# Softmax over 32768 columns: uniform 32 KB chunks, and 896 columns of one late chunk in transfers of seven partitions

## The chip, the core and the metric

The kernel runs on one core of one Trainium2 chip. The metric is the device time of one execution in microseconds; the median of three executions stands for a kernel.

## The reference

```python
batch, seq, vocab = 16, 256, 32768
logits: float32 [16, 256, 32768], temperature = 1.0

scaled = logits / temperature
scaled = scaled - scaled.max(axis=-1, keepdims=True)
exp_scaled = np.exp(scaled)
return (exp_scaled / exp_scaled.sum(axis=-1, keepdims=True)).astype(np.float32)
```

There are 4096 rows of 32768 numbers. 536.87 MB are read and as many are written.

## The kernel before

**Tiling.** Each row is cut into two halves of 16384 columns, and each half sits on a partition of its own, so two neighbouring partitions hold one row. 128 half rows are a group, and there are G = 64 groups. A group is loaded, worked on and stored in two chunks of 8192 columns (`_CW`), each 128 partitions x 32 KB, 4 MB. Six chunk buffers (`X`, `_BUFS`) form a ring, so three groups are in SBUF at a time: group g uses buffers `slots(g)`, that is 2g and 2g + 1 modulo 6.

**Work on a group** (class `Half`). `vector()` runs on VectorE (DVE): for each piece it waits for the load and takes the negated maximum (L123). `scalar()` runs on ScalarE (ACT): it takes the exponential in place and sums it (L168). Then a short chain joins the pieces and the two partitions of a row: a shuffle that swaps neighbours (L134), a minimum (L138), a small exponential (L179), a multiply-add (L142), a reciprocal (L153). At last VectorE scales each piece in place (L157), and a store is issued as soon as its piece is scaled (`stores`).

**Queues.** SyncE (SP) issues all loads, and waits on `st[b]` before it fills a buffer again, until the store of the group before has landed. ScalarE's queue issues the stores of groups 0 to 60 (`stores(act, ...)`), SyncE those of groups 61 to 63. Both queues feed the same 16 DMA engines.

**Edges.** The first and the last group are loaded by `load_edge` in pieces of 4096 columns (`_EDGE`, rows of 16 KB, 2 MB a transfer, L98), all others by `load` (L90). `first()` works on group 0 in whole chunks and waits for both edge pieces of a chunk. `last(G - 1)` works on, and stores, the last group in four pieces of 4096 columns. Groups 1 to 60 run in a loop of `turns` = 20 turns of three groups on VectorE and ScalarE; the rest is written out. All stores go through line L103. At the end SyncE waits for all stores (L255).

The order of SyncE around the change, at the end:

```python
    for c in range(2):
        sp.wait_ge(st[c], (turns + 1) * 16)
        load_edge(G - 1, c, c)
...
    for g in range(G - 3, G):
        last(g).stores(sp, g)
...
    for b in range(_BUFS):
        sp.wait_ge(st[b], total[b])
```

## Time and profile before

| | |
|---|---|
| median of 3 executions | 2488.16 us (2488.12 to 2488.49) |
| the profiled execution: time, span | 2488.27 us, 2486.5 us |
| VectorE busy | 1724.6 us, 69% |
| ScalarE busy | 944.5 us, 38% |
| maximum of a chunk (L123), 126 of 128x8192 | 8.68 us each |
| exponential of a chunk (L168), 126 of 128x8192 | 7.12 us each |
| scaling of a chunk (L157), 126 of 128x8192 | 4.54 us each (mean) |
| 4 MB load, issue to landing (median) | 26.5 us |
| 4 MB store by ScalarE's queue, issue to landing (median) | 48.3 us |
| 4 MB store by SyncE's queue, issue to landing (median) | 33.7 us |

Times in the profile are microseconds from the start of the span. Engines are PE, DVE (VectorE), ACT (ScalarE), POOL (GpSimd) and SP (SyncE); a "q" behind the name (SPq, ACTq) is the engine's sequencer, which waits and issues transfers. L123 is a line of the kernel's file. In a group of instructions, out<-in are the program's names, followed by partitions x elements and type, and xN is how many there are. "Share" or tenths of DMA is the mean over the 16 DMA engines. A transfer of 128 partitions is cut into one packet per row, eight on each engine; each engine writes a four-byte record to the transfer's semaphore when its part is done, so a completion consists of sixteen.

### The profile page before, as it was taken

How to read it: one execution, taken by the hardware profiler on the slowest of the kernel's cores; microseconds unless marked ns; L12 is line 12 of the kernel's file. 1: busy time of each engine (PE TensorE's matmuls, PEld its weight loads, DVE VectorE, ACT ScalarE, POOL GpSimd, SP SyncE). 2: the span in 40 equal slices, each digit the busy share in tenths (PEclk: the TensorE clock that was granted, in tenths of full speed). 3: DMA queues.
4: the chain of work that ended last, by engine and by line, in shares of the span. 5: the costliest groups of instructions: out<-in, count | busy, mean ns of one | idle time of the engine just before them, and what ended most of it. 6: DMA issues, size and time to landing. Idle time of an engine off the chain costs nothing.

```text
span 2486.5 us, 2019 instructions
## 1 busy us (share of the span) xinstructions
DVE 1724.6 (69%) x644; ACT 944.5 (38%) x325; POOL 0.2 (0%) x4
## 2 busy tenths in 40 slices
DVE  6777767767677676676766767667676676766764
ACT  3444333343333433434334343343433434334342
POOL 0000000000000000000000000000000000000000
DMA  9999999999999999999999999999999999999999
GB/s 413 430 435 433 430 438 431 430 438 431 432 436 431 436 432 431 438 430 432 437 430 434 435 430 438 431 430 438 431 432 436 431 436 432 431 438 431 430 437 399
DMA packets 37730, 1073.77 MB, mean 432 GB/s; under 512 B 4192, under 2 KB 4192, under 8 KB 4192
## 3 DMA queue, kind: packets, MB, share of 16 engines
q1 hardware_dynamic: 20160, 562.05, 52.4%
q10 hardware_dynamic: 17568, 511.71, 47.7%
q14 instruction: 2, 0.02, 0.0%
HBM read 536.87 MB, written 536.87 MB: 432 GB/s over the span
## 4 chain that ended last, share of the span: by engine, by line
DMA 58%; DVE 18%; another core or an unknown queue 14%; ACT 8%; issue 1%; SPq 0%; ACTq 0%; DVEq 0%
DMA out_dram<-xs 37%; DMA xs<-in_logits_dram 21%; DVE t L123 11%; ACT xs L168 7%; DVE xs L157 6%; SPq L90 0%; ACT ee L179 0%; DVE t L134 0%; DVE row L153 0%; DVE row L138 0%; DVE junk L142 0%; ACTq L103 0%; SPq L98 0%; DVEq L133 0%
## 5 line engine op out<-in xcount | busy, mean ns | idle before, releaser
L168 ACT ACTIVATE xs<-xs,t 128x8192 f32<-128x8192 f32 (+1 forms) x130 | 912.1, 7016 | 1468.4 <-DVE t L123 1468.4
L123 DVE TENSOR_REDUCE t<-xs 128x1 f32<-128x8192 f32 (+1 forms) x130 | 1110.8, 8551 | 234.0 <-DMA xs<-in_logits_dram 234.0
L157 DVE TENSOR_SCALAR xs<-xs,ee,row 128x8192 f32<-128x8192 f32 (+1 forms) x130 | 576.5, 4478 | 2.3
L134 DVE LOAD_MASK_SELECT t<-t x64 | 0.9, 14 | 470.3 <-ACT xs L168 470.3
L179 ACT ACTIVATE ee<-t,row 128x4 f32<-128x4 f32 x64 | 19.0, 298 | 35.9 <-DVE row L138 35.9
L142 DVE CUSTOM_DVE_ANT_1 junk<-ee,t 128x4 f32<-128x4 f32 x64 | 10.4, 163 | 23.3 <-ACT ee L179 23.3
L168 ACT ACTIVATION_READ_ACCUMULATOR xs<-xs,t 128x1 f32 x130 | 24.3, 187 | 0.0
L153 DVE RECIPROCAL row<-row 128x1 f32<-128x1 f32 x64 | 10.5, 164 | 2.2
L138 DVE TENSOR_REDUCE row<-t 128x1 f32<-128x4 f32 x64 | 10.1, 157 | 2.2
L134 DVE STREAM_SHUFFLE t<-t 128x4 f32<-128x4 f32 x64 | 10.2, 160 | 0.6
L142 DVE DVE_READ_ACCUMULATOR2_ANT row<- 128x1 f32 x64 | 5.3, 82 | 0.0
L168 ACT ACT_TABLE_LOAD x1 | 1.3, 1283 | 0.9 <-SPq L54 0.9
L272 POOL MEMSET const-bfloat16-1.0<- 128x1 bf16 x1 | 0.1, 102 | 0.0
L272 POOL MEMSET const-uint8-127<- 128x1 uint8 x1 | 0.1, 101 | 0.0
L272 POOL MEMSET const-float32-0.0<- 128x1 f32 x1 | 0.1, 99 | 0.2 <-issue 0.2
L272 POOL MEMSET const-float32-1.0<- 128x1 f32 x1 | 0.1, 98 | 0.0
## 6 DMA issues: line engine op xcount, KB each, us to landing
xs<-in_logits_dram SPq DMA_DIRECT2D x124, 4096.0 KB, 26.5
out_dram<-xs ACTq DMA_DIRECT2D x122, 4096.0 KB, 48.3
xs<-in_logits_dram SPq DMA_DIRECT2D x8, 2048.0 KB, 16.1
out_dram<-xs SPq DMA_DIRECT2D x4, 4096.0 KB, 33.7
out_dram<-xs SPq DMA_DIRECT2D x4, 2048.0 KB, 21.9
```

The costliest lines, as they stand in the source:

```text
L123: m = dve.tensor_reduce(out=t[:, k : k + 1], in_=xcols(self.slots[c], s, w), axis=X_, op=A.max, negate=True)
L134: dve.stream_shuffle(out=t[:, 2 * K : 4 * K], in_=t[:, 0 : 2 * K], mask=swap).then_inc(site(tag, "sh"), 1)
L138: dve.tensor_reduce(out=r[:, 0:1], in_=tv[:, :, 0, :], axis=XY, op=A.min).then_inc(site(tag, "mx"), 1)
L142: dve.tensor_tensor_reduce(out=j[:, 0 : 2 * K].rearrange("p (a k) -> p a k", a=2), in0=e[:, 0 : 2 * K].rearrange("p (a k) -> p a k", a=2), ...
L153: dve.reciprocal(out=r[:, 2:3], in_=r[:, 1:2]).then_inc(site(tag, "rc"), 1)
L157: dve.tensor_scalar(out=xs, in0=xs, scalar1=e[:, k : k + 1], scalar2=r[:, 2:3], op0=A.mult, op1=A.mult).then_inc(site(tag, "sc", k), 1)
L168: a = act.activation(out=xs, in_=xs, func=Exp, bias=t[:, k : k + 1], scale=inv_t, accum_out=t[:, K + k : K + k + 1],)
L179: act.activation(out=e[:, 0 : 2 * K].rearrange("p (a k) -> p a k", a=2), in_=tv[:, :, 0, :], func=Exp, bias=r[:, 0:1], scale=-1.0,).then_i ...
L272: nc = _bacc.Bacc("TRN2", target_bir_lowering=False, num_devices=1)
```

## The change

- `load_edge`, `first`, `last` and the pieces of 4096 columns go. All groups are loaded, worked on and stored in whole chunks of 8192 columns.
- The loop of VectorE takes in group 0 and runs 21 turns (groups 0 to 62), then group 63 alone. ScalarE's loop runs 20 turns (groups 0 to 59), and groups 60 to 63 are written out; the store of group 60 stays on its queue.
- SyncE stores groups 61 to 63 as before, but the first chunk of group 62 is split: columns 0 to 7295 go in one transfer of 128 partitions, and columns 7296 to 8191 (896 columns, 3584 B a row) in 19 transfers, 18 of seven partitions and one of two. They have a semaphore of their own (`few`), which only the end waits for.
- The waits at the end stand in another order.

```diff
-_EDGE = 4096
+_FEW = 7
+_FEWCOLS = 896
...
-    turns = (G - 4) // _SETS
+    turns = G // _SETS
...
     for g in range(_SETS):
         for c in range(2):
-            (load_edge if g == 0 else load)(g, c, slots(g)[c])
-    with sp.Fori(1, turns + 1) as i:
+            load(g, c, 2 * g + c)
+    with sp.Fori(1, turns) as i:
         for b in range(_BUFS):
             sp.wait_ge(st[b], i * 16)
             load(i * _SETS + b // 2, b % 2, b)
     for c in range(2):
-        sp.wait_ge(st[c], (turns + 1) * 16)
-        load_edge(G - 1, c, c)
+        sp.wait_ge(st[c], turns * 16)
+        load(G - 1, c, c)
...
     with dve.Fori(1, turns + 1) as i:
         for q in range(_SETS):
-            turn(q, i).vector()
-    for g in range(G - 3, G):
-        last(g).vector()
+            Half(q, i).vector()
+    Half(0, turns + 1).vector()
...
+    last = [(G - 4 + q, Half(q % _SETS, turns + q // _SETS)) for q in range(4)]
+    for g, h in last:
+        h.scalar()
+        if g == G - 4:
+            h.stores(act, g)
...
+    few = nc.alloc_semaphore("few")
+    n_few = 0
+    for g, h in last[1:]:
+        if g != G - 2:
+            h.stores(sp, g)
+            continue
+        sp.wait_ge(site(h.tag, "sc", 0), h.n)
+        b, cut = h.slots[0], _CW - _FEWCOLS
+        sp.dma_start(
+            out=o[bass.ds(g * P, P), 0:cut], in_=X[:, b * _CW : b * _CW + cut]
+        ).then_inc(st[b], 16)
+        for p in range(0, P, _FEW):
+            n = min(_FEW, P - p)
+            sp.dma_start(
+                out=o[bass.ds(g * P + p, n), cut:_CW], in_=X[p : p + n, b * _CW + cut : (b + 1) * _CW]
+            ).then_inc(few, 16)
+            n_few += 1
+        sp.wait_ge(site(h.tag, "sc", 1), h.n)
+        store(sp, g, 1, h.slots[1])
+    sp.wait_ge(few, 16 * n_few)
+    for b in [2, 3, 4, 5, 0, 1]:
+        sp.wait_ge(st[b], 16 * len(range(b, 2 * G, _BUFS)))
```

More of the change, by code (lines that the diff above doesn't have):

```diff
@@ L49 @@
     G = N * 2 // P
-    turns = (G - 4) // _SETS
-    assert turns * _SETS + 4 == G and _BUFS == 2 * _SETS
+    turns = G // _SETS
+    assert turns * _SETS + 1 == G and _BUFS == 2 * _SETS
     swap = [i ^ 1 for i in range(32)]
@@ L55 @@
     X = nc.alloc_sbuf_tensor("xs", [P, _BUFS * _CW], fp32)
-    KM = 4
+    K = 2
     sets = [
         Set(
-            nc.alloc_sbuf_tensor(f"t{q}", [P, 4 * KM], fp32),
-            nc.alloc_sbuf_tensor(f"ee{q}", [P, 2 * KM], fp32),
-            nc.alloc_sbuf_tensor(f"junk{q}", [P, 2 * KM], fp32),
+            nc.alloc_sbuf_tensor(f"t{q}", [P, 4 * K], fp32),
+            nc.alloc_sbuf_tensor(f"ee{q}", [P, 2 * K], fp32),
+            nc.alloc_sbuf_tensor(f"junk{q}", [P, 2 * K], fp32),
             nc.alloc_sbuf_tensor(f"row{q}", [P, 4], fp32),
@@ L69 @@
     st = [nc.alloc_semaphore(f"st{b}") for b in range(_BUFS)]
-    edge = {}
     sites = {}
@@ L78 @@
     sp, dve, act = nc.sync, nc.vector, nc.scalar
-    def spans(step):
-        return [(s, step) for s in range(0, _CW, step)]
-    def xcols(b, s, n):
-        return X[:, b * _CW + s : b * _CW + s + n]
-    def rows(g):
-        return bass.ds(g * P, P)
-    def load(g, c, b):
-        sp.dma_start(
-            out=xcols(b, 0, _CW), in_=x[rows(g), c * _CW : (c + 1) * _CW]
-        ).then_inc(ld[b], 16)
-    def load_edge(g, c, b):
-        for s, n in spans(_EDGE):
-            sem = nc.alloc_semaphore(f"edge{g}_{c}_{s}")
-            edge[g, c, s] = sem
-            sp.dma_start(
-                out=xcols(b, s, n), in_=x[rows(g), c * _CW + s : c * _CW + s + n]
-            ).then_inc(sem, 16)
@@ L102, in store, with chunk @@
-    def store(q, g, c, b, s, n):
-        q.dma_start(
-            out=o[rows(g), c * _CW + s : c * _CW + s + n], in_=xcols(b, s, n)
-        ).then_inc(st[b], 16)
-    class Half:
-        def __init__(self, tag, q, slots, step, landed, n):
-            self.tag, self.set, self.slots, self.n = tag, sets[q], slots, n
-            self.pieces = [(c, s, w) for c in range(2) for s, w in spans(step)]
-            self.K = len(self.pieces)
-            self.landed = landed
+    def chunk(b):
+        return X[:, b * _CW : (b + 1) * _CW]
@@ L116, in vector, with dram, store, __init__ @@
+    def dram(t, g, c):
+        return t[bass.ds(g * P, P), c * _CW : (c + 1) * _CW]
+    def load(g, c, b):
+        sp.dma_start(out=chunk(b), in_=dram(x, g, c)).then_inc(ld[b], 16)
+    def store(q, g, c, b):
+        q.dma_start(out=dram(o, g, c), in_=chunk(b)).then_inc(st[b], 16)
+    class Half:
+        def __init__(self, q, n):
+            self.tag, self.set, self.n = f"q{q}", sets[q], n
+            self.slots = [2 * q, 2 * q + 1]
         def vector(self):
             t, e, j, r = self.set.parts()
-            K, n, tag = self.K, self.n, self.tag
+            n, tag = self.n, self.tag
@@ L119, in vector @@
             tv = t[:, 0 : 4 * K].rearrange("p (a b k) -> p a b k", a=2, b=2)
-            for k, (c, s, w) in enumerate(self.pieces):
-                for sem, value in self.landed(c, s):
-                    dve.wait_ge(sem, value)
+            for k in range(K):
+                dve.wait_ge(ld[self.slots[k]], n * 16)
                 m = dve.tensor_reduce(
-                    out=t[:, k : k + 1], in_=xcols(self.slots[c], s, w), axis=X_, op=A.max, negate=True
+                    out=t[:, k : k + 1], in_=chunk(self.slots[k]), axis=X_, op=A.max, negate=True
@@ L154, in vector @@
             dve.wait_ge(site(tag, "rc"), n)
-            for k, (c, s, w) in enumerate(self.pieces):
-                xs = xcols(self.slots[c], s, w)
+            for k in range(K):
+                xs = chunk(self.slots[k])
                 dve.tensor_scalar(
@@ L162, in scalar @@
             t, e, j, r = self.set.parts()
-            K, n, tag = self.K, self.n, self.tag
+            n, tag = self.n, self.tag
             tv = t[:, 0 : 4 * K].rearrange("p (a b k) -> p a b k", a=2, b=2)
-            for k, (c, s, w) in enumerate(self.pieces):
-                xs = xcols(self.slots[c], s, w)
+            for k in range(K):
+                xs = chunk(self.slots[k])
                 act.wait_ge(site(tag, "m", k), n)
@@ L187, in stores @@
         def stores(self, q, g):
-            for k, (c, s, w) in enumerate(self.pieces):
+            for k in range(K):
                 q.wait_ge(site(self.tag, "sc", k), self.n)
-                store(q, g, c, self.slots[c], s, w)
-    def slots(g):
-        return [2 * g % _BUFS, (2 * g + 1) % _BUFS]
-    def fine(g):
-        return lambda c, s: [(edge[g, c, s], 16)]
-    def coarse(n16):
-        return lambda c, s: [(ld[b], n16)] if s == 0 else []
-    def first():
-        return Half("f", 0, slots(0), _CW, lambda c, s: [(edge[0, c, p], 16) for p, _ in spans(_EDGE)], 1)
-    def turn(q, i):
-        b = slots(q + 1)
-        return Half(f"q{q}", (q + 1) % _SETS, b, _CW, lambda c, s: [(ld[b[c]], i * 16)], i)
-    def last(g):
-        b = slots(g)
-        if g == G - 1:
-            return Half("l2", g % _SETS, b, _EDGE, fine(g), 1)
-        return Half(f"l{g}", g % _SETS, b, _CW, lambda c, s: [(ld[b[c]], (g // _SETS + (b[c] > 1)) * 16)], 1)
+                store(q, g, k, self.slots[k])
     for g in range(_SETS):
         for c in range(2):
-            (load_edge if g == 0 else load)(g, c, slots(g)[c])
-    with sp.Fori(1, turns + 1) as i:
+            load(g, c, 2 * g + c)
+    with sp.Fori(1, turns) as i:
         for b in range(_BUFS):
@@ L223 @@
     for c in range(2):
-        sp.wait_ge(st[c], (turns + 1) * 16)
-        load_edge(G - 1, c, c)
-    first().vector()
+        sp.wait_ge(st[c], turns * 16)
+        load(G - 1, c, c)
     with dve.Fori(1, turns + 1) as i:
         for q in range(_SETS):
-            turn(q, i).vector()
-    for g in range(G - 3, G):
-        last(g).vector()
-    f = first()
-    f.scalar()
-    f.stores(act, 0)
-    with act.Fori(1, turns + 1) as i:
+            Half(q, i).vector()
+    Half(0, turns + 1).vector()
+    with act.Fori(1, turns) as i:
         for q in range(_SETS):
-            h = turn(q, i)
+            h = Half(q, i)
             h.scalar()
-            h.stores(act, i * _SETS + (q + 1 - _SETS))
-    for g in range(G - 3, G):
-        last(g).scalar()
-    for g in range(G - 3, G):
-        last(g).stores(sp, g)
-    total = [0] * _BUFS
-    for g in range(G):
-        for b in slots(g):
-            total[b] += 16 * (_CW // _EDGE if g == G - 1 else 1)
-    for b in range(_BUFS):
-        sp.wait_ge(st[b], total[b])
+            h.stores(act, i * _SETS + (q - _SETS))
+    last = [(G - 4 + q, Half(q % _SETS, turns + q // _SETS)) for q in range(4)]
[25 more added lines that the diff above has]
+        sp.wait_ge(st[b], 16 * len(range(b, 2 * G, _BUFS)))
 _INS = ['logits', 'temperature']
```

## The prediction

> **What bounds the kernel now.** I read the page's shares and its DMA line first, then the DMA view of the last 26 us, then the timeline of the last group, then SyncE's instructions and waits.

> ```profile
> span 2486.5 us, 2019 instructions
> DVE 1724.6 (69%) x644; ACT 944.5 (38%) x325; POOL 0.2 (0%) x4
> DMA  9999999999999999999999999999999999999999
> DMA packets 37730, 1073.77 MB, mean 432 GB/s; under 512 B 4192, under 2 KB 4192, under 8 KB 4192
> ```

> No engine is busy for more than 69%, while the 16 DMA engines are at nine tenths or more in all 40 slices. 1073.77 MB is what the task must read and write, so nothing in the change can take bytes away. The kernel is a DMA stream with a start and an end, and what can be moved is the evenness of the end. This is the DMA view for 2464 to 2490 us (40 slices of 0.65 us):

> ```profile
> DMA  9999999999999999999999999999100000000000
> GB/s 504 479 454 454 429 403 403 403 403 403 403 403 454 454 454 479 504 403 479 403 403 403 403 403 403 403 429 403 76 25 25 25 0 0 0 0 0 0 0 0
> ```

> The stream runs at full rate to 2482.2 us, and then three slices move 25 GB/s: 432 / 16 is 27, so one engine works alone. The packet records give the same: thirteen engines end their last packet between 2482.15 and 2482.41 us, the others at 2482.84, 2483.41 and 2484.84. The last one sets the end. Its delay is not born at the end: among the sixteen completions of each DMA the last comes 0.33 us after the first at 211 us of the span, 0.79 at 676, 1.61 at 1450 and 2.48 at 2225. That is one engine that steadily loses about 1 ns in each us. The other two appear between 2350 and 2400 us, where the only two instruction fetches of the span (8 KB each, 2355.0 and 2383.1 us) fall.

> The last group and SyncE's issues (timeline), and then SyncE's instructions of the store line and its waits:

> ```profile
> 0.95 1.91 SPq L98 DMA_DIRECT2D xs<-in_logits_dram  x4
> ...
> 2418.73 9.00 DVE L157 TENSOR_SCALAR xs<-xs,ee,row 128x8192 f32<-128x8192 f32 x2
> 2427.64 17.39 DVE L123 TENSOR_REDUCE t<-xs 128x1 f32<-128x4096 f32 x4
> ...
> 2445.07 3.71 ACT L168 ACTIVATE xs<-xs,t 128x4096 f32<-128x4096 f32 x1 [0.53 <-DVE t L123]
> ...
> 2450.18 9.38 DVE L157 TENSOR_SCALAR xs<-xs,ee,row 128x4096 f32<-128x4096 f32 x4
> ```

> ```profile
> L103 SPq DMA_DIRECT2D out_dram<-xs x8: 332/332/430, 2411.4 to 2459.6; - x8
> ```

> ```profile
> SPq L255 <- DMA out_dram<-xs: 25.2, 1, 25.2
> ```

> The last store is issued at 2459.6, and SyncE then waits 25.2 us for stores that have all been issued: at the end there is a backlog, and the compute of the last group lies under it.

> **The change, part by part.** The base is the profiled execution: 2488.27 us, 1.8 us around its span. It lies 0.11 us over the median of 2488.16.

> *32 KB rows instead of 16 KB.* Alone in the queues, two 2 MB stores take 2 x 4.855 us (completions at the end) and one 4 MB store 9.66 us, 0.05 us less; at the head two 2 MB loads take 2 x 4.89 us against 9.71, 0.07 less. Two chunks at the head, two last loads (by the head's rows) and two last stores give 0.14 + 0.14 + 0.10 = 0.38 us off every engine. From both kinds of packet a row costs about 6 ns and its bytes 27.27 GB/s.

> *The head and the loop.* The first maximum waits for both edge halves of its chunk already (13.10 us), so a whole load costs it nothing. The first group enters the loop. In the loop the same instructions, waits and transfers run, and DVE has 234.0 us of waits for loads there. Nothing.

> *The last group in two pieces.* DVE ends its scaling of group 62 at 2427.73 and its two maxima at 2445.0; ACT's second exponential ends at 2445.0 + 7.12 + 0.19 = 2452.3 (2448.9 before), the small chain to the scaling takes 1.3 as before, and the two scalings of 4.5 end at 2458.1 and 2462.6, 3 us later than before. The stream needs the first of these stores when it has all else behind it: 2482.4 less two stores of 9.66 is 2463.1, less 0.25 (rows, above) and 1.06 (below) is 2461.8 on the engines that get there first. From issue to first packet the head shows 1.0 us (0.95 to 1.97), so the data flow from 2459.2: 2.6 us of cover remain. Hidden; were the cover gone, each us too late would be a us on all engines.

> *Nineteen narrow stores.* The last 896 columns are 3584 B a row. All engines lose eight such ends of rows: 8 x 3584 B at 27.27 GB/s = 1.05 us. Engines 0 to 6 get 18 rows of 3584 B (the first two 19, by the last transfer of two partitions): 18 x (131 + 6) ns = 2.47 us. Net -1.05 us on the upper nine, +1.42 (two of them +1.56) on the lower seven. No row of before is as small, so 137 ns is an extrapolation. It is bounded from below by the bytes alone (131 ns) and from above by a row that also waits for its own completion: the last packet ends at 2484.84 and SyncE wakes at 2485.33, 0.49 us, so 0.62. I take 137, since two row sizes give the line and every four-byte completion record of the tail is followed by data of the next transfer on the same engine 6 ns later.

> *Their issue.* SyncE issues back to back at 0.48 us (1.91 us for four). After 2423.3 the wide part and nineteen more take to about 2432.7, where 2427.8 stood for the second store of group 62, which is queued behind them. That store is needed at about 2452.3, so 19.6 us of cover remain; a narrow issue would have to take 1.5 us to use it up, and I have no row of a narrow issue.

> *Sum.* If the late engine is among the upper nine, it ends at 2484.84 - 0.38 - 1.05 = 2483.4, and the lower ones at 2482.41 - 0.38 + 1.56 = 2483.6: 1.25 us gained. If one of the two others (0.4 and 1.0 us late) is a lower one, the end is 2484.0 or 2484.5 and the gain 0.8 or 0.4. I take 1.1: 2488.27 - 1.1 - 0.11 = 2487.1 us, a change of 0.04%. A measurement of this kernel can tell about 0.2% (5 us) from no change, so the forecast is no change.

> The trace has no engine numbers, so only the count speaks: 9 of 16 engines are relieved. [...]

> **The rivals.**

> *The late engine is a lower one.* Then 2484.84 - 0.38 + 1.42 is 2485.9: +1.0 us, 2489.2. Speaking for it: the count, 7 of 16.

> *Neighbouring rows share a way out of SBUF.* In the wide stores each engine drains eight rows of its own at 27 GB/s. If that pace is that of a path which eight partitions share, seven engines that read seven neighbours share few paths: 2.5 on average where paths take partitions by fours, 1.75 by eights. The 458.8 KB then take 6.8 or 9.7 us instead of 2.47, and the low engines end at 2482.41 - 0.38 - 1.05 + 6.8 = 2487.8 (2490.7): 2491.2 or 2494.1 us. The trace cannot exclude it, since each wide store reaches all partitions at once. [...]

> *Each narrow store waits for its own completion*, the one that ends slower. Its place is the lower seven engines between the two stores of group 62. At 0.62 us a transfer 18 take 11.2 us, and these engines end at 2481.0 + 11.2 = 2492.2: +7.4 us, 2495.5. It passes 0.2% from 0.49 us a transfer on (8.9 us / 18). For it: in the trace two completions on an engine and queue are never closer than 4.8 us. Against it: the 6 ns above.

> *The narrow stores are spread over all engines.* Then only the 0.38 us stay, less 8 x 6 ns: 2487.8.

> **How the numbers follow.** Forecast 0.40 and late engine below 0.30 (9 to 7, of 0.70); shared paths 0.17, of which 0.03 for eights; own completion, or an issue over 1.5 us, 0.08; spread 0.03; a gain over 5 us, for which I see no place, 0.02. Within 0.2% lie 0.40 + 0.30 + 0.14 + 0.03 = 0.87, slower 0.03 + 0.08 = 0.11, faster 0.02. The range from 2486.5 (both gains whole, 1.43 us, and the medians' spread) to 2491.7 (paths by fours, and half a us) holds the 0.87.

> **What would show it.** Right: 3584 B packets of about 137 ns; the slices of one engine's 25 GB/s gone or halved, the last packet at 2483.4 to 2484.5; SyncE's nineteen issues done by 2435. Shared paths: narrow packets of 300 ns and more and some seven engines busy after the others. Own completion: gaps of 0.5 us between them. Late engine below: the 25 GB/s slices longer by 1 to 2.5 us. An issue of the last group's first store after 2461, or a dip of all engines before 2480, would break the cover.

## The result: 4 us slower, and the profile after

The changed kernel takes 2492.27 us (median of 22 runs, 2491.83 to 2493.85) against 2488.23 us (22 runs, 2488.02 to 2488.67): a ratio of 1.0016, 95% interval 1.001 to 1.0022. That is 0.16%, inside the 0.2% that the prediction called no change, but above its range (2486.5 to 2491.7) and on the other side of its number (2487.1).

The page after: the sums, the table loads of ScalarE, and the DMA issues by line (engine, count, KB each, median us to landing).

```profile
span 2490.2 us, 2044 instructions
DVE 1724.0 (69%) x640; ACT 968.1 (39%) x340; POOL 0.2 (0%) x4
DMA packets 37121, 1073.77 MB, mean 431 GB/s; under 512 B 4224, under 2 KB 4224, under 8 KB 4352
...
L150 ACT ACT_TABLE_LOAD x20 | 25.7, 1283 | 196.0 <-DVE xs L139 194.9
...
out_dram<-xs SPq DMA_DIRECT2D x1, 3648.0 KB, 34.0
out_dram<-xs SPq DMA_DIRECT2D x18, 24.5 KB
out_dram<-xs SPq DMA_DIRECT2D x1, 7.0 KB
```

The bytes are the same and the stream still binds. The 128 packets that "under 8 KB" counts more than "under 2 KB" are the narrow rows. Of the 4.0 us, 3.6 lie in the span (2490.1 us at the median against 2486.5) and 0.4 outside it: 2.2 us are outside the span now, 1.8 before. Inside the span the time has gone in three places, and the first is 70 us before the end. The stretches of 4 us around the last group's loads, before and then after (duration; DVE, ACT, POOL busy; clock; DMA share; GB/s, where a packet counts at its start):

```profile
2414.00:2418.00 4.00, 0.33 (x3) 3.44 (x3) 0.00 (x0) 1.00 0.98 418
2418.00:2422.00 4.00, 3.61 (x4) 0.29 (x1) 0.00 (x0) 1.00 1.02 434
2422.00:2426.00 4.00, 4.00 (x2) 0.00 (x0) 0.00 (x0) 1.00 1.08 463
2426.00:2430.00 4.00, 4.00 (x2) 0.00 (x0) 0.00 (x0) 1.00 0.91 393
```

```profile
2414.00:2418.00 4.00, 0.33 (x3) 3.44 (x3) 0.00 (x0) 1.00 1.03 401
2418.00:2422.00 4.00, 3.81 (x4) 0.09 (x1) 0.00 (x0) 1.00 0.94 401
2422.00:2426.00 4.00, 4.00 (x2) 0.00 (x0) 0.00 (x0) 1.00 0.98 262
2426.00:2430.00 4.00, 4.00 (x2) 0.00 (x0) 0.00 (x0) 1.00 1.07 459
```

In these 16 us the stream moves 6.09 MB after (the four rates by 4 us) against 6.83 MB before. If each packet's bytes are spread over its own duration and set against 16 engines of 27.1 GB/s (32 KB in 1.21 us), the engines lose 0.64 us (mean of an engine) in 2414 to 2418 and 1.60 us in 2422 to 2430, and less than 0.1 us before. I call this the loss of a stretch from here on. SyncE's timeline shows what happens there, before and then after:

```profile
2394.22 17.14 SPq L98 DMA_DIRECT2D xs<-in_logits_dram  x4
2411.40 12.23 SPq L103 DMA_DIRECT2D out_dram<-xs  x3
```

```profile
2394.02 19.70 SPq L87 DMA_DIRECT2D xs<-in_logits_dram  x2
2413.76 0.91 SPq L90 DMA_DIRECT2D out_dram<-xs  x2
2423.10 0.33 SPq L214 DMA_DIRECT2D out_dram<-xs  x1
2423.47 9.18 SPq L219 DMA_DIRECT2D out_dram<-xs  x19
```

The last load (chunk 1 of group 63) was issued at 2410.55 before and is issued at 2413.37 now, because the store of group 60 that it waits for lands 2.8 us later (2412.91 in place of 2410.08, by the last of its sixteen completions). The load of chunk 0, the only other work in the queues, ends from 2414.11 us on, and a new load's first packet comes 1.0 us after its issue: at 2414.4 only 10 of 16 engines have a packet under way, and their first packets take 1.3 to 2.0 us in place of 1.2. The stores of groups 61 and 62 can't help, since they stand behind the waiting load on SyncE.

The other two places are at the end. There is the loss of 0.33 us in 2454 to 2462 around the narrow rows, and there is the late engine, which ends its last wide row of the split chunk at 2456.64 and its last narrow row at 2459.55, and has no gap from there to the end. The tail (40 slices of 0.65 us from 2464) shows it alone:

```profile
GB/s 605 353 504 403 403 403 454 555 252 605 202 655 202 655 252 555 454 403 403 454 504 302 605 202 605 252 605 252 605 353 101 252 101 0 50 50 0 0 0 0
```

Nine engines end from 2483.49 to 2484.26, six at 2485.7 to 2486.1, and one at 2488.60. Six and one: the late engine is among the seven that carry the narrow rows.

### The profile page after: what moved, and what is told of

Its sections match the earlier page's. It is cut to its first block, busy times and chain, and to the rows that moved or that the text cites. A ratio compares the mean times of both kernels' runs of the same rounds, so it can differ in the third digit from the quotient of the medians.

```text
span 2490.2 us, 2044 instructions
## 1 busy us (share of the span) xinstructions
DVE 1724.0 (69%) x640; ACT 968.1 (39%) x340; POOL 0.2 (0%) x4
## 2 busy tenths in 40 slices
DMA  9999999999999999999999999999999999999999
DMA packets 37121, 1073.77 MB, mean 431 GB/s; under 512 B 4224, under 2 KB 4224, under 8 KB 4352
## 4 chain that ended last, share of the span: by engine, by line
DMA 58%; DVE 18%; another core or an unknown queue 14%; ACT 8%; issue 1%; SPq 0%; ACTq 0%; DVEq 0%
DMA out_dram<-xs 37%; DMA xs<-in_logits_dram 21%; DVE t L105 11%; ACT xs L150 8%; DVE xs L139 6%; SPq L87 0%; ACT ee L161 0%; DVE t L116 0%; DVE row L135 0%; DVE row L120 0%; DVE junk L124 0%; ACTq L90 0%; DVEq L115 0%; DVE row L124 0%
## 5 line engine op out<-in xcount | busy, mean ns | idle before, releaser
L150 ACT ACTIVATE xs<-xs,t 128x8192 f32<-128x8192 f32 x128 | 911.5, 7121 | 1252.9 <-DVE t L105 1252.9
L105 DVE TENSOR_REDUCE t<-xs 128x1 f32<-128x8192 f32 x128 | 1110.6, 8681 | 234.0 <-DMA xs<-in_logits_dram 234.0
L139 DVE TENSOR_SCALAR xs<-xs,ee,row 128x8192 f32<-128x8192 f32 x128 | 576.1, 4543 | 2.3
L150 ACT ACT_TABLE_LOAD x20 | 25.7, 1283 | 196.0 <-DVE xs L139 194.9
```

The costliest lines, as they stand in the source:

```text
L105: m = dve.tensor_reduce(out=t[:, k : k + 1], in_=chunk(self.slots[k]), axis=X_, op=A.max, negate=True)
L139: dve.tensor_scalar(out=xs, in0=xs, scalar1=e[:, k : k + 1], scalar2=r[:, 2:3], op0=A.mult, op1=A.mult).then_inc(site(tag, "sc", k), 1)
L150: a = act.activation(out=xs, in_=xs, func=Exp, bias=t[:, k : k + 1], scale=inv_t, accum_out=t[:, K + k : K + k + 1],)
```

## The experiments

Times are medians, each beside the kernel before, timed on the same chip (e1 to e4 on one chip, e5 to e8 on a second, e9 to e11 on a third). The 95% intervals reach some 2.2 us to each side, and many of the differences below are no larger than that. They are read where no execution of one kernel overlaps those of the other, as for e1, e2, e3, e6, e7 and e10 against the kernel before, and by the packets.

**e1 and e2: the two halves of the change.** e1 puts the narrow stores into the kernel before:

```diff
     for g in range(G - 3, G):
-        last(g).stores(sp, g)
+        h = last(g)
+        if g != G - 2:
+            h.stores(sp, g)
+            continue
+        ... (the wide store of 7296 columns and nineteen narrow ones, as in the change)
```

> The kernel before with the nineteen narrow stores alone (edges of 4096 columns kept). Theory 1: the late engine is one of the seven low ones (+1.4 to +1.5 us), and the run of narrow issues is what slowed all engines at 2422 to 2426 us in the changed kernel (1.6 us of engine time) and at 2454 to 2460 (0.3 us): about 2488.2 + 3.4 = 2491.6 us, with packets of over 2 us just after 2423. Theory 2: the slow packets at 2422 to 2426 belong to the last group's whole loads: about 2488.2 + 1.8 = 2490.0 us and no such packets here.

Measured: 2491.53 us (2491.16 to 2491.76, 11 runs) against 2488.30; ratio 1.0013, interval 1.0004 to 1.0022. The total is theory 1's, the place is not: no slow packets after 2423; instead the stretch 2450 to 2458 loses 0.96 us. The late engine's narrow rows take longer than the trace of the change shows: 3.73 us from its last wide row (2455.25) to the last narrow one (2458.98).

e2 is the change without the narrow stores:

```diff
     for g, h in last[1:]:
-        if g != G - 2:
-            h.stores(sp, g)
-            continue
-        ... (wide store, nineteen narrow stores)
+        h.stores(sp, g)
```

> The changed kernel without the narrow stores (first chunk of group 62 stored whole). Theory 1: only the dry queue at the last load's issue is left (0.64 us of engine time at 2414 to 2418), less 0.1 to 0.4 us for fewer rows: about 2488.6 us, and no slow packets at 2422 to 2426. Theory 2: those stay, and the time is about 2490.3 us.

Measured: 2490.39 us (2490.11 to 2491.67, 11 runs) against 2488.30; 1.0009, 1.0 to 1.0018. Theory 2 holds. With not one narrow transfer in the kernel the same stretches are slow, 0.78 us lost in 2414 to 2418 and 1.31 in 2422 to 2430:

```profile
2414.00:2418.00 4.00, 0.33 (x3) 3.44 (x3) 0.00 (x0) 1.00 1.06 401
2418.00:2422.00 4.00, 3.72 (x4) 0.18 (x1) 0.00 (x0) 1.00 0.91 393
2422.00:2426.00 4.00, 4.00 (x2) 0.00 (x0) 0.00 (x0) 1.00 0.99 287
```

So the uniform chunks alone cost 2.1 us (1.7 in the span, 0.4 outside it as in the changed kernel) and the narrow stores alone 3.2.

**e3: work for the queues while SyncE waits.**

```diff
-        if g == G - 4:
+        if g <= G - 3:
             h.stores(act, g)
...
-    for g, h in last[1:]:
+    for g, h in last[2:]:
```

> The changed kernel, with the two stores of group 61 issued by ScalarE's queue, where they needn't wait behind the last load. Theory 1: the engines have work when the last load is issued, the loss of 0.64 us at 2414 goes, the narrow stores' costs stay: about 2491.6 us. Theory 2 (all losses before 2430 come of the whole last load meeting empty queues): 2.2 us go, about 2490.0 us.

Measured: 2491.28 us (2490.98 to 2491.45, 11 runs) against 2488.30; 1.0012, 1.0003 to 1.0021. Both losses before 2430 are gone (no stretch from 2394 to 2450 over 0.05 us), so both belong to the queue that runs dry, as theory 2 says. The time fell by 1.0 us and not 2.2. The late engine, which sets the end, ends its last wide row 2.26 us sooner than in the changed kernel (2454.38), but then takes 3.81 us for its narrow rows in place of 2.91; why is open. There is a second loss that doesn't reach the end: the last load now shares the engines with group 61's stores and lands at 2440.0 where VectorE had been ready for it at 2436, group 63's first store is issued at 2461.82 and comes too late, and the stretch 2462 to 2466 loses 0.40 us. That is the cover of 2.6 us that the prediction counted for this store, used up, but only on engines ahead of the late one, which has no gap from 2458.19 to its end at 2487.23.

**e4: which engine is late.** The last 1040 columns of the chunk go in transfers of 1, 2, ... 15 partitions (and one more of 8), each count with two row sizes of its own:

```diff
-        for p in range(0, P, _FEW):
-            n = min(_FEW, P - p)
...
+        p = 0
+        for n in list(range(1, 16)) + [8]:
+            w = 128 + 32 * n
+            for lo, hi in ((cut, cut + w), (cut + w, _CW)):
```

> The changed kernel with the last 1040 columns of that chunk in transfers of 1, 2, 3 ... 15 partitions (and one more of 8), each count with a row size of its own (two transfers: 128 + 32n columns and the rest), so the sizes that an engine carries name it. The late engine runs its narrow rows about 2.5 us after the others. Theory 1: it carries those of 3 to 7 partitions and up but not those of 1 and 2, since in the changed kernel it had 18 narrow rows and not 19, so it is one of engines 2 to 6. The rival, that it is engine 7 or above and the count of rows was misread, has it carry only rows of 8 partitions and more, or none.

Measured (one run, 2493.44 us): the late engine ends its last wide row at 2456.27, over 2 us after all others (2454.12), and then carries rows of 1152 and 3008 B, 1280 and 2880, 1408 and 2752, 1536 and 2624 and so on: the transfers of 5 partitions and up, and none of 1 to 4. The trace has no engine numbers; here engines are numbered from 0 in the order in which the transfers of 1, 2, 3 and more partitions take them in, and so counted the late one is engine 4. That every transfer of n partitions runs on the first n of this order is my assumption; the sizes of rows show it for the late engine alone. In the changed kernel the narrow stores leave 128 completion records, 18 x 7 and 2; the late engine has 18 rows of 3584 B and not 19, so it was not one of the two engines of the last transfer there either. This run names the engine on its own chip. On the other two chips the late engine isn't among engines 0 to 3: in e7 and e9, where four engines carry the narrow rows, it has none.

**e5 and e6: why the queue is dry.** On e2, chunk 0 (e5) or chunk 1 (e6) of the last group is loaded in two transfers of 4096 columns:

```diff
     for c in range(2):
         sp.wait_ge(st[c], turns * 16)
-        load(G - 1, c, c)
+        if c == 0:      # e6: 1
+            for s in range(2):
+                lo = c * _CW + s * (_CW // 2)
+                sp.dma_start(out=X[:, lo : lo + _CW // 2], in_=x[...]).then_inc(half[s], 16)
+        else:
+            load(G - 1, c, c)
```

> Uniform chunks without narrow stores, but the last group's chunk 0 is loaded in two transfers of 4096 columns (16 KB rows), chunk 1 whole. Theory A: both losses of e2 (0.8 us at 2414 to 2418, 1.3 us at 2422 to 2428) come of a queue that is dry when chunk 1's load is issued, and it is dry since 32 KB rows of chunk 0's load take half of the turns, where 16 KB rows leave two thirds of the bytes to the store that SyncE waits for. Then both go: 2488.3 us, SyncE issues chunk 1's load near 2410.5. Theory B: the second loss belongs to a whole chunk's load with stores behind it in the same queue: 1.3 us stay, 2489.5 us.

> The mirror of the run above: the last group's chunk 0 is loaded whole, chunk 1 in two transfers of 4096 columns. Theory A: the queue is dry as in e2, both losses stay: 2490.4 us, load issue near 2413.4. Theory B: the loss at 2414 stays, the one at 2422 to 2428 goes: 2489.1 us.

Measured: e5 2488.20 us (11 runs) against 2488.24, ratio 0.9999, 0.999 to 1.0008; e6 2490.13 us (11 runs), 1.0008, 0.9999 to 1.0017. Theory A: rows of 16 KB in the load of chunk 0 undo the loss, in chunk 1 they don't. (Outside the span both have 1.8 us, as the kernel before, so 0.4 us of what e5 wins back against e2 isn't the queue's.) SyncE's timeline in e6 still has the late issue:

```profile
2394.07 0.34 SPq L85 DMA_DIRECT2D xs<-in_logits_dram  x1
2413.44 0.82 SPq L191 DMA_DIRECT2D xs<-in_logits_dram  x2
```

The packets show the way it works. From 2399 to 2407 us, when chunk 0's load on SyncE's queue and group 60's store on ScalarE's compete, the kernel before starts 65 packets of 16 KB of the load (1.06 MB) and 67 of 32 KB of the store (2.20 MB); the changed kernel 55 (1.80 MB) and 50 (1.64 MB) of 32 KB each. Put in order by engine, a row of the store and a row of the load alternate one by one in both kernels. So beside rows half as long the store gets two thirds of the bytes (2.20 of 3.26 MB), beside equal rows about half (1.64 of 3.44): from 2398.5 us on, five rows of the load go ahead of the store's completion on each engine, and each takes 0.61 us before and 1.21 after. That is 3.0 us more, and the landing moves by 2.8. Before, the store lands earlier, SyncE goes on earlier, and the load has 4 us left as cover.

e5's profiled execution took 2492.36 us, unlike its ten others (2487.8 to 2488.3), and bears this out by accident: there the late engine was 8.5 us behind the first where it was 2.5 in the kernel before, the store of group 60's first chunk landed at 2397.1 instead of 2393.7, chunk 1's load was issued at 2413.43, and both losses (0.78 and 1.40 us) were there again. (The other 2 us are the late engine's, which ends 5.0 us behind in place of 2.7. No trace of an e5 execution near 2488 us was kept.)

**e7 and e9: engines 0 to 3 alone.** The kernel before with 448 columns on the four engines below the late one; in e7 by transfers of four partitions, in e9 by one of 124 and one of 4 (the lines below are against e1):

```diff
-_FEW = 7
-_FEWCOLS = 896
+_FEW = 4            # e9: _FEWS = (124, 4); e10: (119, 7, 2), 896 columns
+_FEWCOLS = 448
...
-        for p in range(0, P, _FEW):
-            n = min(_FEW, P - p)
+        p = 0               # e9, e10, e11 only
+        for n in _FEWS:
...
+            p += n
```

> The kernel before (edges kept) with narrow stores of four partitions and 448 columns: engine 4, the late one by e4's signature, is relieved by 8 rows of 1792 B (0.53 us), engines 0 to 3 carry 32 such rows (about 2.45 us, net +1.9). If an engine's own rows decide: 0.5 us gained, 2487.8 us, and the stretch of one engine's 25 GB/s at the end shorter. If the relief is lost to the narrow rows' traffic, as 1.1 us of it was for the upper engines in e1: 2488.3 to 2489.3 us.

> As e7 (kernel before, 448 columns on engines 0 to 3), but the 32 transfers of four partitions become two: one of 124 partitions, which four engines carry with 31 rows each (4 is the largest divisor of 124 up to 16), and one of 4. The same rows lie on the same engines. If e7's 3 us came of the many transfers (their rows took 180 ns instead of 74 once some 16 were done), the rows now take about 72 ns, the late engine 4 is relieved by 0.53 us and engines 0 to 3 end with it: 2487.8 us. If rows of 1792 B as such cost that: 2491 us as in e7.

Measured: e7 2491.31 us (2491.21 to 2491.68, 11 runs) against 2488.24, 1.0012, 1.0003 to 1.0021; e9 2488.38 us (2488.23 to 2488.78, and one of the 11 runs at 2491.79) against 2488.21, 1.0002, 0.9993 to 1.0011. e7 lies above both of its expected times. The same rows on the same engines cost 2.9 us less in two transfers than in 32. In e7, 60 of the 128 rows take 74 ns and 68 take 175 ns on average; in e9 all take 74. The tails (from 2464, e7 and then e9) show four engines or so busy alone (126 GB/s, five rows of 16 KB in a slice of 0.65 us), for 5 us and for 2.5:

```profile
GB/s 403 454 454 454 454 403 429 403 429 403 429 403 429 429 403 429 479 429 529 403 429 429 429 403 403 429 403 126 126 126 126 151 126 126 76 25 0 0 0 0
```

```profile
GB/s 353 403 429 454 403 454 479 454 403 429 403 429 454 403 429 403 429 454 429 454 454 429 454 429 403 429 429 151 126 126 101 25 0 0 0 0 0 0 0 0
```

e9 gained nothing either. By the completion records one of the engines was itself 1.1 us late before, and with narrow rows on top it took the late engine's place at the end. That the 124 partitions lie on four engines was an assumption too, and this tail agrees with it.

**e10: the narrow rows of the change in three transfers** (119, 7 and 2 partitions; diff above).

> As e1 (kernel before with 896 columns on engines 0 to 6), but with three transfers, of 119, 7 and 2 partitions, instead of nineteen: again 18 rows of 3584 B on each low engine (19 on the first two). If the many transfers cost the shared 1 us (all engines lost 0.96 us at 2450 to 2458 in e1), only the late low engine's extra rows stay: 18 x 0.138 - 1.05 = +1.4 us, 2489.7 us. If small rows read by few engines cost it: 2491.5 us as in e1.

Measured: 2490.39 us (2490.21 to 2490.62, 11 runs) against 2488.21; 1.0008, 0.9999 to 1.0017. That is between its two expected times, and 1.1 us less than e1 (2.2 over the kernel before, e1 3.2). The stretch 2450 to 2458 loses 0.1 us instead of 0.96, and the late engine takes 3.24 us for its 18 narrow rows instead of 3.73; less the 1.05 us of the wide rows, that is the whole 2.2. The tails of e1 and then e10:

```profile
GB/s 378 403 378 429 403 479 403 429 403 429 454 479 454 403 429 429 403 429 403 454 403 403 454 403 454 429 479 429 277 252 126 76 25 25 25 25 25 0 0 0
```

```profile
GB/s 429 403 403 429 403 454 429 403 454 454 479 403 429 454 403 429 403 429 403 429 479 403 454 429 479 429 252 176 176 176 101 50 25 25 25 0 0 0 0 0
```

In e10 seven engines are busy after the others (176 GB/s, seven rows of 16 KB a slice). In both the end is one engine alone, the late one with its 18 rows. In e1 the upper nine end later (full rate for two more slices), so their relief had been lost.

**e8: an even load in small transfers of neighbours**, on the kernel before (as e1):

```diff
-_FEW = 7
+_FEW = 16
```

> The kernel before with the 896 columns in eight transfers of sixteen neighbouring partitions: every engine carries one row of each, so the load is even and the late engine gets no more than before. If neighbours share paths out of SBUF (by fours: sixteen rows on four paths), each transfer takes 57 KB / 109 GB/s = 0.53 us instead of 0.14 and all engines lose about 3.1 us: 2491.4 us. If rows of 3584 B or closely spaced completions as such cost time, all lose 1 us or more. If neither: 2488.4 us.

Measured: 2488.80 us (2488.47 to 2489.15, 11 runs) against 2488.24; 1.0002, 0.9993 to 1.0011. Of 128 rows 119 take the 140 ns that they take anywhere, and from 2452.5 to 2453.1 thirteen or fourteen engines run such rows at once. Paths shared by fours, at the pace that the prediction gave them, are out; eight transfers of one row an engine cost at most some 0.6 us (the executions overlap with those of the kernel before), less than the 1 us of the third case.

**e11: e9 with fewer columns**, to beat the kernel before:

```diff
-_FEWCOLS = 448
+_FEWCOLS = 256
```

> As e9, with 256 columns instead of 448 on engines 0 to 3. In e9 one of the four low engines, itself 1.1 us late from an instruction fetch before, ended last (its 32 rows of 70.5 ns net +1.7 us), and took the place of the relieved engine 4. With rows of 1024 B the low engines gain only 32 x 43 ns - 0.30 = 1.06 us, the late engine is relieved by 0.30 us, and should be last again: 0.3 us faster than the kernel before, 2487.9 us. If the relief of the late engine doesn't reach the end: 2488.2 us.

Measured: 2488.29 us (2487.84 to 2488.50, 11 runs) against 2488.22; 1.0, 0.9991 to 1.0009. No gain that these runs can tell. No version beats the kernel before.

## Why the prediction was wrong, point by point

**What bounds the kernel** was right: the stream, with the compute under it, and an end that one engine draws out.

**"The head and the loop. Nothing."** Right in time. ScalarE's table load moved into the loop (20 instead of 1, 25.7 us busy), which I hadn't seen, but 19 of them fall into waits for VectorE.

**"32 KB rows instead of 16 KB", -0.38 us: the step that failed with no rival to cover it.** I costed row size by the overhead of a packet alone. In e2 the first engines end 1.8 us later though 2.1 us are lost, so up to 0.3 us of it is there. But row size also set how the two queues shared an engine (a third of the bytes for the load with rows of 16 KB, about half with 32 KB), and through it the landing of a store, the issue of the last load behind it, and a queue that ran dry: 2.1 us lost, +1.7 us in the span (e2), undone by e5. I named the cover of the last stores and of SyncE's nineteen issues, and not that of the last load, which had 4 us of its neighbour's load over it. The prediction's sign for it, a dip of all engines before 2480, did come, at another place than the one it watched.

**"If the late engine is among the upper nine": false.** It carries narrow rows in the changed kernel, e1 and e10, and on e4's chip it is engine 4. This second step that failed had been named as a rival, with a chance little below the forecast's. The sum of that rival, 18 rows less eight ends, +1.42 us, was somewhat small: the 18 rows took 2.91 us, which is 1.9 net, and the late engine is about 2.5 us behind its six neighbours at the end, as it was behind most engines before.

**"Nineteen narrow stores", 137 ns a row: right for the row, wrong for the transfers.** 125 of 128 rows take 140 ns. The late engine's 18 took 162 ns on average, as one of them took 0.49 us. What I missed is a cost of many small transfers beyond their rows: 1.1 us for nineteen against three (e1, e10), 2.9 us for 32 against two (e7, e9). The rival "each narrow store waits for its own completion" was the nearest idea and too strong: from some 15 rows an engine on, a transfer cost 0.1 us more in e7, not the rival's 0.62. Its place was wrong too, for the upper engines lose as well (e1).

**"Neighbouring rows share a way out of SBUF": false here.** No run shows paths that take partitions by fours or by eights. By fours e8 would have been 3.1 us slower, by the estimate in its expectation; it measured 0.6, with 119 of 128 rows at 140 ns. For stores of this size the measurement decides against them. (This rival's two times leave out the 0.11 us that the other sums take off; with it they are 2491.1 and 2494.0.)

**"Their issue"** and **the last group in two pieces** were right: 9.18 us for nineteen (0.48 each), the second store of group 62 issued at 2432.70, and the last two stores at 2457.83 and 2462.29 (2458.1 and 2462.6 forecast):

```profile
2427.44 17.27 DVE L105 TENSOR_REDUCE t<-xs 128x1 f32<-128x8192 f32 x2
2432.70 29.92 SPq L90 DMA_DIRECT2D out_dram<-xs  x3
...
2453.26 9.00 DVE L139 TENSOR_SCALAR xs<-xs,ee,row 128x8192 f32<-128x8192 f32 x2
```

**The sum.** The late engine's rows give it. The uniform chunks made e2's span 1.7 us longer, and the late engine's narrow rows cost 1.9 net: that is the 3.6 us by which the changed kernel's span grew. The other 0.4 us lie outside the span, which the prediction kept at 1.8 us around it: 2.2 in the changed kernel, e2, e3 and e4, and 1.8 in the kernel before, e5 and e6. Why is open. Alone the two halves give 2.1 + 3.2 = 5.3 us, more than the 4.0 measured, because in e1 the late engine's narrow rows took 3.73 us and not 2.91, and its wide rows before them ended some 0.6 us late (2455.25, where the kernel before less 1.05 gives 2454.64). Why the same rows take 2.91, 3.24, 3.73 or 3.81 us on it stays open.

So does the second part of the dry queue's loss. Some 8 us after the restart the last two rows of the late load take up to 2.3 us each in place of 1.21 (in e6 the last rows of 16 KB take about 1 us in place of 0.61), in every run that ran dry and in no other. It isn't only the engines that ran dry: the late engine, which still had rows of chunk 0, had no gap, and two of its rows took 1.43 and 3.39 us then. Nothing in the traces names what they wait for.

## What to carry to other kernels

When a kernel is bound by its DMA stream, look for every place where a queue's next transfer waits for another queue's landing, and write down how much work is still queued when that wait ends; here rows of 32 KB in place of 16 KB raised a load's share from a third of the bytes to about half and moved that moment by 2.8 us. Before load is shifted between DMA engines to relieve a late one, find out which engine it is: row sizes that name the engine do it in one run, for that chip. Put the shifted rows into few transfers: here nineteen cost 1.1 us more than three, and 32 cost 2.9 us more than two. One transfer of 124 partitions (e9) or of 119 (e10) left four engines or so, or seven, busy alone at the end (126 and 176 GB/s, five and seven rows of 16 KB a slice).
